# RWKV substitution: rows of the 16-blocks spread over their partitions through DRAM instead of by shuffles

## The chip, the cores and the metric

One core of a Trainium2 chip runs the whole program. The metric is the device time of one execution in microseconds, as the median of several runs. The engines are PE (TensorE, matrix products), PEld (its weight loads), DVE (VectorE), ACT (ScalarE), POOL (GpSimd) and SP, which here only issues transfers. Each engine runs its own instructions in the order in which they were placed on it; it waits at an instruction until what that needs is there, and everything behind it on that engine waits too.

## What is computed

One residual block over 256 tokens of width 2048, in f32: RMS norm, one wide input projection, RWKV-7 time mixing (16 heads of 64) and latent attention side by side, gates and an output projection, then a gated MLP and an input embedding. The change lies in the RWKV part. Cut to what matters of the reference:

```python
def rwkv7_scan(r, decay, k, v, kk, a):
    def step(state, inp):                      # 256 steps, state 64 x 64 per head
        r_t, w_t, k_t, v_t, kk_t, a_t = inp
        sa = jnp.einsum('bhvk,bhk->bhv', state, -kk_t)
        state = (state * w_t[:, :, None, :]
                 + sa[..., None] * (kk_t * a_t)[:, :, None, :]
                 + v_t[..., None] * k_t[:, :, None, :])
        y_t = jnp.einsum('bhvk,bhk->bhv', state, r_t)
        return state, y_t
    ...
u = rms_norm(h, pre_mix_norm[i])
z = u @ w_in[i]
z_rw, z_mla, z_gate = jnp.split(z, (RW_COLS, RW_COLS + MLA_COLS), axis=-1)
...
mix = (g_rw * (y_rw @ w_branch_rw[i]) + g_mla * (y_mla @ w_branch_mla[i])) @ w_out[i]
```

## The kernel before

**The scan in chunks.** The 256 steps are done as 4 chunks of 64 (`NCH`, `C`). Inside a chunk the steps depend on each other through a 64 x 64 triangular matrix for each head, `n`. Its inverse is needed. It is built from the inverses of its 16 x 16 blocks on the diagonal: those come by substitution, column after column, and the larger blocks by products (`ph`, `px`).

**Tiles.** A pair is two heads, on partitions 0 to 63 and 64 to 127. `rw_pair(J, j, ...)` is a generator for pair `j` of 8. Two pairs run side by side as one round, `par` 0 and 1, so there are four rounds. The substitution is done once for both: the second pair (`par == 1`) issues it for a tile that holds both. `dg` (128 partitions x 128 elements) holds the diagonal blocks of both pairs and all four chunks: every 16 partitions are the 16 rows of a block, and the 16 elements in a row stand side by side. `xc` of the same shape takes the inverse and starts as the identity.

**Rows for everybody.** To eliminate in column `t`, every partition of a block needs all rows of that block. They are kept in `rp16`, 16 x 128 elements on each partition. Fifteen instructions fill it: shuffle `i` copies row `i` of each 16-partition group to the 16 partitions of its group. Row 15 isn't needed and holds ones. The columns then are two DVE instructions each, a product into `pd` and a sum into `xc`; each depends on the one before. `pd` shares its memory with `dg` (tag `dg`, one buffer).

**Dense work between.** The matrix products of the projections are another generator, `dense_work`. It yields once for each block of 128 rows of weights: 6 matmuls of 256 columns, the planner's unit. `rw_pair` yields after each of its steps a length in such units, and the loop behind `duo` advances `dense_work` by as many. So `SUB = 1.56` units stand behind each step of the substitution, `STEP = 2.4` behind other steps. This sets the order in which instructions are made; a scheduler then places them on each engine by what is ready when, with evacuations ahead.

**Weights.** `wchunk` loads 128 x 1024 f32 on SP's queue into `raw` (3 buffers). For each half, ACT rounds it into `hi` (L148) and DVE subtracts for the remainder `lo` (L149), in 5 buffers each. One such half serves two units, 12 matmuls (L183 to L185: hi times hi, hi times lo, lo times hi). So DVE has to make one `lo` for each half-chunk that TensorE goes through, and whatever holds DVE holds these.

**Names around it.** L848 makes `dg` ready for the substitution. L866 and L867 split weights of the pair's output gate (`lgs`, from `lwr`), L735 those of the next pair (`lws`). L992, L999 and L162 finish the pair before (`yf`, `yrw`). L362 mixes neighbouring tokens of a new projection (`z`). L871 and L888 are the first steps behind the columns (`Xc`, `YH`), L893 and L897 the products' halves on DVE. L730 is ACT's load of `lwr` for a later pair.

Of the kernel before, what the change touches and what calls it, by code (L numbers as in the profile page):

```python
# [8 lines left out]
F32 = mybir.dt.float32  # L9
# [7 lines left out]
P = 128  # L17
# [8 lines left out]
NH = 8  # L26
DS = float(np.exp(-0.5))

STEP, CHUNK, SUB = 2.4, 2.8, 1.56


NONE, READY, FREE, HOLD, AHEAD, TAIL = 0, 2, 3, 5, 6, 7
# [76 lines left out]
def hybrid_block(tc, A):  # L109
    nc = tc.nc  # L110
# [199 lines left out]
    es_e = ExitStack()  # L310
# [7 lines left out]
    def e2(nm, shape=None, dt=F32):  # L318
        return mp.tile(shape or [P, 2 * T], dt, name=nm, tag="e2", bufs=17)
# [261 lines left out]
    for i in range(2):  # L581
        p = slice(64 * i, 64 * i + 64)
# [22 lines left out]
    for j in range(2):  # L605
        ps = run(dense(cq, [A["w_q"][4 + j]], 4))
        o, b = e2("upo", [P, 2, T]), e2("qps", [P, 2, T])
# [94 lines left out]
    es_e = ExitStack()  # L702
# [2 lines left out]
    Xbs, krs = [[ep.tile([P, NCH, 2, C], F32, name=f"{nm}{i}") for i in range(2)] for nm in ("Xb", "kb")]  # L705
    for n in Xbs + krs:
        nc.gpsimd.memset(n[:], 0.0)
    rp16 = ep.tile([P, 16, 2 * NCH * 16], F32, name="rp16")
    nc.gpsimd.memset(rp16[:, 15, :], 1.0)

# [3 lines left out]
    def rw_pair(J, j, k, r, v):  # L714
        par = j % 2
# [95 lines left out]
        n = ep.tile([P, NCH, C], F32, name=f"n{par}", bufs=1)  # L811
# [29 lines left out]
        dg, xc = J["dg"], J["xc"]  # L841
# [3 lines left out]
        if par == 1:  # L845
            d8, x8 = [a[:].rearrange("p r c j -> p (r c) j") for a in (dg, xc)]
            act(x8, i16, AF.Copy)
            tt(out=d8, in0=i16, in1=d8, op=ALU.subtract)  # L848
        yield NONE, SUB

        for o in range(0, 15, 3):
            if par == 1:
                for i in range(o, o + 3):
                    nc.vector.stream_shuffle(out=rp16[:, i, :], in_=dg[:].rearrange("p r c j -> p (r c j)"),
                                             mask=[i] * 16 + [16 + i] * 16)
            yield NONE, SUB
        for t in range(1, 16):
            if par == 1:
                pd = ep.tile([P, 2 * NCH, 16], F32, name="pd", tag="dg", bufs=1)
                r8 = rp16[:].rearrange("p i (q j) -> p q i j", j=16)  # L860
                tt(out=pd[:, :, 0:t + 1], in0=x8[:, :, 0:t + 1], in1=r8[:, :, 0:t + 1, t], op=ALU.mult)
                nc.vector.tensor_reduce(out=x8[:, :, t], in_=pd[:, :, 0:t + 1], axis=AX.X, op=ALU.add)
            yield NONE, SUB
        lgs = ep.tile([P, 3, P], F32R, name="lgs", bufs=2)
        act(lgs[:, 0:2, :], lwr[:, 2:4, :], AF.Copy)
        tt(out=lgs[:, 2, :], in0=lwr[:, 2, :], in1=lgs[:, 0, :].bitcast(F32), op=ALU.subtract)  # L866
# [47 lines left out]
        for h in range(2):  # L914
# [4 lines left out]
            o = pb[:, 0:T].rearrange("p (c n) -> p c n", c=NCH)  # L919
# [15 lines left out]
        for c in range(NCH):  # L935
# [3 lines left out]
            o = lambda i, h, hs: pc[hs, i * P + h * C:i * P + h * C + C]  # L939
# [97 lines left out]
    def duo(q):  # L1037
        while len(zz[q]) < 3:
            next(work)
        J = {}  # L1040
        return [rw_pair(J, 2 * q + c, *[z[:, c, :] for z in zz[q]]) for c in range(2)]
# [176 lines left out]
    with tc.tile_pool(name="fw", bufs=2) as fw, tc.tile_pool(name="psu", bufs=3, space=PSUM, reuse_waits="tile") as psu:  # L1218
# [30 lines left out]
        for n, (j, q) in enumerate([(j, q) for q in range(4) for j in range(3)] + [(j, q) for j in range(3, NFF) for q in range(4)]):  # L1249
# [12 lines left out]
            if (j, q) == (0, 3):  # L1262
# [5 lines left out]
                r = st[:, 26:28]  # L1268
# [177 lines left out]
```

## Time and profile before

| | |
|---|---|
| median of 3 runs | 1561.18 us (1561.16 to 1561.9) |
| the profiled execution | 1560.39 us, span 1558.6 us |
| granted TensorE clock | 0.997 |
| shuffles, L854 | 60, 297 ns median, 228.1 to 505.0 us |
| the column's product, L861 | 60, 285 ns median, 233.1 to 519.9 us |
| the column's sum, L862 | 60, 226 ns median |
| mean DMA rate | 183 GB/s |

The profile is of one execution and so compares with its own 1560.39 us. Times in it are from the start of its span. Engines overlap: an engine's idle time costs only where another waits for it. A matmul is listed with its full length of some 0.28 us though the next starts 0.12 us behind it, so that short waits of TensorE are covered by busy time.

### The profile page before, as it was taken

Reading aid. Unit: us, or ns where it says so; the run is one execution under the profiler, and the core shown is the slowest. Engines: PE = TensorE matmul, PEld = TensorE weight load, DVE = VectorE, ACT = ScalarE, POOL = GpSimd, SP = SyncE. Lnnn points to the kernel's source line nnn. Section 1 sums busy time; section 2 is a strip of 40 time slices with the busy share of each in tenths; the row PEclk is TensorE's granted clock in tenths of the full one; section 3 lists DMA queues with packets and bytes.
Section 4 is the critical chain, followed back from the end, with each engine's and each line's share of the span. In section 5 each row is a group of like instructions: output and inputs, shape, how many; then the busy total and the mean of one; then the engine's idle time right before and its main releaser. Section 6 shows DMA issues by size and latency. Waiting matters only on the chain.

```text
span 1558.6 us, 29636 instructions
## 1 busy us (share of the span) xinstructions
PE 1538.0 (99%) x10850; PEld 1388.3 (89%) x10850; DVE 1182.2 (76%) x2670; ACT 942.1 (60%) x1944; POOL 60.9 (4%) x125
## 2 busy tenths in 40 slices
PE   9999999999999999999999999999999999999997
PEld 9989999999999999887888888888888888888886
DVE  7896687898989776557787777777777655777866
ACT  7686756566565555456766555555655555776653
POOL 0000201101011102000000000000000000000000
PEclk9999999999999999999999999999999999999998
DMA  8654555454444546865656555565655666666564
GB/s 304 192 172 141 154 173 164 138 171 129 147 150 136 160 153 200 306 199 167 203 174 205 198 181 202 179 203 179 206 181 190 175 192 195 197 197 191 166 200 148
DMA packets 80482, 285.19 MB, mean 183 GB/s; under 512 B 9040, under 2 KB 10320, under 8 KB 80336
## 3 DMA queue, kind: packets, MB, share of 16 engines
q1 hardware_dynamic: 77760, 279.48, 56.3%
q10 hardware_dynamic: 2576, 3.81, 0.7%
q8 instruction: 85, 1.39, 0.4%
q14 instruction: 61, 0.50, 0.1%
HBM read 281.16 MB, written 2.10 MB: 182 GB/s over the span
## 4 chain that ended last, share of the span: by engine, by line
PE 89%; DVE 6%; ACT 2%; DMA 1%; issue 1%; DVEq 0%; ACTq 0%
PE d L170 21%; PE d L174 11%; PE d L183 9%; PE d L185 8%; PE d L184 8%; PE o L196 7%; PE o L198 6%; PE o L200 6%; PE e L196 2%; PE e L198 2%; PE e L200 2%; DVE lo L149 2%; ACT hi L148 1%; DMA raw<-in_w_in 1%; PE tr L237 0%
## 5 line engine op out<-in xcount | busy, mean ns | idle before, releaser
L149 DVE TENSOR_TENSOR lo<-raw,hi 128x512 fp32r<-128x512 f32 x684 | 461.0, 690 | 213.9 <-ACT hi L148 208.5
L148 ACT CAST hi<-raw 128x512 fp32r<-128x512 f32 x684 | 410.7, 619 | 297.9 <-PE o L200 97.9
L183 PE MATMUL d<-uT,hi 128*128 128x256 f32 x1072 | 307.7, 287 | 0.7 <-ACT hi L161 0.6
L170 PE MATMUL d<-u,highs 128*128 128x512 f32 x1312 | 305.5, 390 | 0.0
L185 PE MATMUL d<-uT,lo 128*128 128x256 f32 x1072 | 300.5, 280 | 0.7 <-DVE lo L162 0.2
L184 PE MATMUL d<-uT,hi 128*128 128x256 f32 x1072 | 299.6, 279 | 0.1
L170 PEld LDWEIGHTS d<-u,highs 128*128 128x128 f32 x1312 | 243.3, 188 | 48.9
L148 ACT CAST highs<-raw 128x512 fp32r<-128x512 f32 x328 | 186.8, 616 | 115.0 <-DMA raw<-in_w_up 80.3
L183 PEld LDWEIGHTS d<-uT,hi 128*128 128x128 f32 x1072 | 201.7, 188 | 2.8 <-ACT hi L161 0.8
L185 PEld LDWEIGHTS d<-uT,lo 128*128 128x128 f32 x1072 | 201.5, 188 | 2.1 <-DVE lo L149 1.1
L184 PEld LDWEIGHTS d<-uT,hi 128*128 128x128 f32 x1072 | 201.7, 188 | 0.4 <-DVE uT L290 0.3
L149 DVE TENSOR_TENSOR hi<-raw,highs 128x512 fp32r<-128x512 f32 x164 | 112.7, 688 | 76.8 <-PE d L174 58.8
L174 PE MATMUL d<-u,lo 128*128 128x256 f32 x752 | 117.7, 280 | 0.0
L149 DVE TENSOR_TENSOR lo<-raw,highs 128x512 fp32r<-128x512 f32 x164 | 112.0, 684 | 0.0
L174 PE MATMUL d<-u,hi 128*128 128x256 f32 x656 | 103.3, 279 | 0.0
L174 PEld LDWEIGHTS d<-u,lo 128*128 128x128 f32 x752 | 101.7, 188 | 0.8
L174 PEld LDWEIGHTS d<-u,hi 128*128 128x128 f32 x656 | 91.5, 188 | 3.5
L198 PE MATMUL o<-lo,fsplit 128*128 128x512 f32 x264 | 88.6, 389 | 0.0
L196 PE MATMUL o<-hi,fsplit 128*128 128x512 f32 x264 | 88.5, 389 | 0.0
L200 PE MATMUL o<-hi,fsplit 128*128 128x512 f32 x264 | 88.4, 389 | 0.0
L1228 ACT ACTIVATE cy<-d 128x512 f32<-128x512 f32 x44 | 26.2, 597 | 67.8 <-PE d L174 67.8
L198 PEld LDWEIGHTS o<-lo,fsplit 128*128 128x128 f32 x264 | 49.6, 188 | 10.7 <-DVE lo L149 0.3
(389 smaller groups left out, 2550.9 us busy)
## 6 DMA issues: line engine op xcount, KB each, us to landing
raw<-in_w_up SPq DMA_DIRECT2D x176, 512.0 KB, 4.3
raw<-in_w_in SPq DMA_DIRECT2D x133, 512.0 KB, 3.6
raw<-in_w_down SPq DMA_DIRECT2D x88, 512.0 KB, 4.3
raw<-in_w_out SPq DMA_DIRECT2D x32, 512.0 KB, 4.4
raw<-in_w_pg SPq DMA_DIRECT2D x32, 512.0 KB, 3.6
raw<-in_w_bm SPq DMA_DIRECT2D x16, 512.0 KB, 3.7
raw<-in_w_br SPq DMA_DIRECT2D x16, 512.0 KB, 3.7
raw<-in_w_kv SPq DMA_DIRECT2D x8, 512.0 KB, 3.6
```

What stands on the lines that cost most here:

```text
L148: nc.scalar.copy(hi[:], raw[:, c:c + 512])
L149: tt(out=lo[:], in0=raw[:, c:c + 512], in1=hi[:].bitcast(F32), op=ALU.subtract)
L170: mm(ps[:, c, :], hi(i, col, P), mov[i][2], start=first and x == 0 and i == 0, stop=False)
L174: mm(ps[:, c, 0:T], lo(i, col, P), mov[i][0], start=False, stop=last and x == len(parts) - 1 and i == len(mov) - 1)
L183: mm(ps[:, c, :], hi(i, col, P), mov[i][:, 0:T], start=f, stop=False)
L184: mm(ps[:, c, :], hi(i, col, P), mov[i][:, T:2 * T], start=False, stop=False)
L185: mm(ps[:, c, :], lo(i, col, P), mov[i][:, 0:T], start=False, stop=l)
L196: mm(b[:], h, hi(i, g * 512, 512), start=f, stop=False)
L198: mm(b[:], h, lo(i, g * 512, 512), start=False, stop=False)
L200: mm(b[:], x, hi(i, g * 512, 512), start=False, stop=l)
L1228: act(y[:], ps[:, :, 0:T], AF.Copy)
```

## The change

The fifteen shuffles go. ACT issues a transfer that writes `dg` to DRAM (`rows16`, 128 x 128 f32, 64 KB). POOL issues one that reads it back: each partition gets the 15 x 128 elements of the first fifteen rows of its block in one piece of 7,680 bytes, and the 16 partitions of a block all read the same piece. Where five steps of the substitution held the shuffles, six empty steps follow. The steps of the columns are 1.45 units long and no longer 1.56.

```diff
-STEP, CHUNK, SUB = 2.4, 2.8, 1.56
+STEP, CHUNK, SUB, COL = 2.4, 2.8, 1.56, 1.45
...
+    rows16 = es_e.enter_context(tc.tile_pool(name="dr", bufs=1, space=bass.MemoryType.DRAM)).tile([P, P], F32, name="rows16")
     rp16 = ep.tile([P, 16, 2 * NCH * 16], F32, name="rp16")
...
         yield NONE, SUB
-
-        for o in range(0, 15, 3):
-            if par == 1:
-                for i in range(o, o + 3):
-                    nc.vector.stream_shuffle(out=rp16[:, i, :], in_=dg[:].rearrange("p r c j -> p (r c j)"),
-                                             mask=[i] * 16 + [16 + i] * 16)
+        if par == 1:
+
+            nc.scalar.dma_start(rows16[:], dg[:].rearrange("p r c j -> p (r c j)"))
+            nc.gpsimd.dma_start(rp16[:, 0:15, :].rearrange("p i n -> p (i n)"),
+                                bass.AP(rows16.tensor, rows16.offset, [[16 * P, 8], [0, 16], [1, 15 * P]]))
+        for _ in range(6):
             yield NONE, SUB
         for t in range(1, 16):
             if par == 1:
...
-            yield NONE, SUB
+            yield NONE, COL
```

The new lines make later line numbers one higher: L848 becomes L849, L861 L862, L862 L863, L148 and L149 stay. In the rows below `rp_2510` and `rp_2513` are `rp16`, and `rows_2512` is `rows16`.

DVE in the first round, from `dg` made ready to the first columns, before:

```order
L848 TENSOR_TENSOR dg<-cst,dg 128x128
L149 TENSOR_TENSOR lo<-raw,hi 128x512
L854 STREAM_SHUFFLE rp_2510<-dg 128x128 x5
L149 TENSOR_TENSOR lo<-raw,hi 128x512
L854 STREAM_SHUFFLE rp_2510<-dg 128x128 x4
L149 TENSOR_TENSOR lo<-raw,hi 128x512
L854 STREAM_SHUFFLE rp_2510<-dg 128x128 x4
L149 TENSOR_TENSOR lo<-raw,hi 128x512
L854 STREAM_SHUFFLE rp_2510<-dg 128x128 x2
L861 TENSOR_TENSOR pd<-xc,rp_2510 128x8x2
L862 TENSOR_REDUCE xc<-pd 128x8
L149 TENSOR_TENSOR lo<-raw,hi 128x512
```

And after:

```order
L849 TENSOR_TENSOR dg<-cst,dg 128x128
L149 TENSOR_TENSOR lo<-raw,hi 128x512 x5
L362 SCALAR_TENSOR_TENSOR z_3270<-d,vec,z_3270 128x255
L149 TENSOR_TENSOR lo<-raw,hi 128x512
L362 SCALAR_TENSOR_TENSOR z_3270<-d,vec,z_3270 128x255
L862 TENSOR_TENSOR pd<-xc,rp_2513 128x8x2
L863 TENSOR_REDUCE xc<-pd 128x8
L862 TENSOR_TENSOR pd<-xc,rp_2513 128x8x3
L149 TENSOR_TENSOR lo<-raw,hi 128x512
```

Six `lo` stand between `dg` and the first column where four stood, and the first column now needs the read. In the later rounds L999 (now L1000) has also moved ahead of the first column.

ACT in the second round, from before the write to the loads of `lwr`, after:

```order
L148 CAST hi<-raw 128x512 x2
L853 DMA rows_2512<-dg 128x128
L148 CAST hi<-raw 128x512
L991 ACTIVATE yf<-pm,vec 128x256 x2
L148 CAST hi<-raw 128x512
L361 ACTIVATE z_4723<-d,omu 128x256
L148 CAST hi<-raw 128x512
L361 ACTIVATE z_4723<-d,omu 128x256
L866 ACTIVATE lgs<-lwr 128x256 x2
L148 CAST hi<-raw 128x512
L731 DMA lwr<-in_w_lora 128x512
L148 CAST hi<-raw 128x512
```

Before, the same piece read:

```order
L148 CAST hi<-raw 128x512 x3
L990 ACTIVATE yf<-pm,vec 128x256 x2
L148 CAST hi<-raw 128x512
L361 ACTIVATE z_4740<-d,omu 128x256
L148 CAST hi<-raw 128x512
L361 ACTIVATE z_4740<-d,omu 128x256
L865 ACTIVATE lgs<-lwr 128x256 x2
L148 CAST hi<-raw 128x512
L730 DMA lwr<-in_w_lora 128x512
```

The write stands between two casts and waits for DVE's L849; the rest of ACT's order is the same.

POOL in the first round, after; ahead of the change the row of the DMA was not there:

```order
L798 COPY bk_2912<-bk_2912 64x4x64
L798 COPY bk_2916<-bk_2916 64x4x64
L854 DMA rp_2513<-rows_2512 128x1x1920
L901 COPY Xb_2502<-Xc_3557 32x4x32 x4
L901 COPY Xb_2503<-Xc_3563 32x4x32 x4
```

The read stands ahead of POOL's copies of the substitution's result (before: L900). SP's order of transfers is unchanged.

## The prediction

> **What bounds the kernel now.** I read the page first, then the stretches around the four substitutions, then the DVE's groups and its order in time there, and last the landings of transfers. A count after x is how often a row stands.
>
> ```profile
> span 1558.6 us, 29636 instructions
> ...
> PE 1538.0 (99%) x10850; PEld 1388.3 (89%) x10850; DVE 1182.2 (76%) x2670; ACT 942.1 (60%) x1944; POOL 60.9 (4%) x125
> ...
> PE 89%; DVE 6%; ACT 2%; DMA 1%; issue 1%; DVEq 0%; ACTq 0%
> ```
>
> TensorE is the bound over the whole program: 89% of the chain that ended last is its own. A change on DVE pays only where the chain leaves TensorE for DVE. The profiled execution took 1560.39 us with a span of 1558.6; the median of the runs is 1561.18, so I add the differences to that. The table of stretches (columns: length; then busy time of PE, PEld, DVE, ACT and POOL; clock, DMA share, GB/s) cuts out the four rounds, one for each two pairs of heads, from the end of L848 to the transposes behind the columns:
>
> ```profile
> 227.60:252.00 24.40, 24.40 (x212) 24.40 (x210) 23.35 (x86) 11.25 (x21) 0.00 (x0) 1.00 0.57 175
> 317.40:347.00 29.60, 29.14 (x377) 28.39 (x374) 27.71 (x103) 15.73 (x34) 0.00 (x0) 1.00 0.62 181
> 408.00:439.00 31.00, 29.88 (x381) 28.39 (x379) 29.22 (x104) 15.73 (x31) 0.18 (x1) 1.00 0.59 186
> 499.60:529.00 29.40, 29.01 (x378) 28.46 (x380) 26.28 (x96) 16.63 (x31) 0.00 (x0) 1.00 0.52 169
> sum 114.40, PE 112.43 PEld 109.64 DVE 106.56 ACT 59.34 POOL 0.18; mean PE 28.11 PEld 27.41 DVE 26.64 ACT 14.84 POOL 0.04
> ```
>
> In the rounds DVE is busy 106.6 of 114.4 us: here, and hardly elsewhere, it is as full as TensorE. Yet TensorE idles only 114.40 - 112.43 = 1.97 us in all four, none of it in round 1. So relief of DVE can return about 2 us, a little more if waits shorter than one matmul stand hidden in busy time. That is below 0.2% (3.1 us), which is about what a measurement of this kernel tells from no change.
>
> What DVE does in round 1, by groups:
>
> ```profile
> L149 DVE TENSOR_TENSOR lo<-raw,hi 128x512 fp32r<-128x512 f32 x18 | 12.1, 679 | 0.0
> L861 DVE TENSOR_TENSOR pd<-xc,rp 128x16 f32<-128x16 f32 (+14 forms) x15 | 4.3, 289 | 0.4
> L854 DVE STREAM_SHUFFLE rp<-dg 128x128 f32<-128x128 f32 x15 | 3.5, 294 | 0.0
> L862 DVE TENSOR_REDUCE xc<-pd 128x8 f32<-128x16 f32 (+14 forms) x15 | 3.4, 227 | 0.3
> ```
>
> **The change, part by part.**
>
> *Shuffles removed.* 15 shuffles a round; successive ones start about 0.21 us apart though each lasts 0.294, so a round saves 15 x 0.21 = 3.1 us of DVE, 12.4 us in all. What of it reaches the end is bounded by the 1.97 us above. Little does even so: the six steps in which DVE is now free stand before the first column, and DVE cannot work ahead there, because lo waits for hi and hi for TensorE to give a buffer back. These ACT rows show that pace:
>
> ```profile
> 228.05 0.62 ACT L148 CAST hi<-raw 128x512 fp32r<-128x512 f32 x1 [0.46 <-PE d L184]
> ...
> 229.45 0.62 ACT L148 CAST hi<-raw 128x512 fp32r<-128x512 f32 x1 [0.78 <-PE d L184]
> ```
>
> One half-chunk, the work of one hi and one lo, lasts TensorE 1.40 us, which is two of the planner's units; a SUB is 1.09 us.
>
> *Columns closer.* 15 x 1.45 = 21.75 units of cover instead of 23.4, with the same columns. A column costs DVE 289 + 227 = 516 ns; per half-chunk there are 1.38 columns instead of 1.28, so DVE falls behind by 0.05 us more on each of some 11, 0.5 us a round; but the columns end 0.8 half-chunk earlier and DVE's load is lighter behind them. I take zero and keep +0.5 a round for the range. The sixth step balances it: 6 x 1.56 + 21.75 + 1.56 = 32.67 units a round against 32.76.
>
> *The round trip added.* ACT issues a write of 64 KB, POOL waits for it and issues a read of 128 x 7,680 B = 983 KB, and the first column waits for that. Neither transfer has a row. Nearest rows (KB each, median us from issue to landing) and the weight queue's packets, MB and share:
>
> ```profile
> q1 hardware_dynamic: 77760, 279.48, 56.3%
> ...
> raw<-in_w_in SPq DMA_DIRECT2D x133, 512.0 KB, 3.6
> ...
> lwr<-in_w_lora ACTq DMA_DIRECT2D x8, 256.0 KB, 3.0
> ...
> gbc<-in_g_pm SPq DMA_DIRECT2D x2, 512.0 KB, 5.3
> ...
> gple<-in_g_pl SPq DMA_DIRECT2D x2, 512.0 KB, 7.1
> ...
> out<-h ACTq DMA_DIRECT2D x4, 256.0 KB, 2.2
> ```
>
> The write: 2.2 (out, the only writes to DRAM) to 3.0 us (lwr, on ACT's queue beside the weights); I take 2.3. The read: 279.48 MB in 56.3% of 1558.6 us is 318 GB/s with all engines busy, so the 459 KB beyond a 512 KB transfer add 1.4 us: 3.6 + 1.4 = 5.0 at least, 7.1 + 1.4 = 8.5 at most, and 5.3 + 1.4 = 6.7 by gbc, which like this read repeats a piece of DRAM over partitions while weights flow. I take 6.7. POOL's own start: below nothing beyond the landing times, above 1.3 us, the longest issue in the trace (below); I take 0.5. So the data lands 9.5 us after L848 ends, with ends at 7.2 and 12.8.
>
> ```profile
> L1134 SPq DMA_DIRECT2D gple<-in_g_pl x2: 432/872/1312, 645.9 to 648.6; - x2
> ```
>
> The Trainium skill's "DMA: Bandwidth & Descriptors", Anatomy of one DMA, fits a GpSimd transfer with 2.0 us plus bytes over 436 GB/s. By that the read would take 4.3 us, the landing would be near 7, and this sum would be zero. The trace speaks against it: for 512 KB the fit gives 3.2 us, the rows 3.6 to 7.1.
>
> *When it is too late.* DVE in order of time in rounds 1 to 4: L848, the first column, and the lo that the new order puts behind its first columns.
>
> ```profile
> 227.26 0.29 DVE L848 TENSOR_TENSOR dg<-cst,dg 128x128 f32<-128x128 f32 x1
> ...
> 233.10 0.19 DVE L861 TENSOR_TENSOR pd<-xc,rp 128x16 f32<-128x16 f32 x1
> ...
> 236.37 0.68 DVE L149 TENSOR_TENSOR lo<-raw,hi 128x512 fp32r<-128x512 f32 x1
> ...
> 317.10 0.28 DVE L848 TENSOR_TENSOR dg<-cst,dg 128x128 f32<-128x128 f32 x1
> ...
> 325.12 0.18 DVE L861 TENSOR_TENSOR pd<-xc,rp 128x16 f32<-128x16 f32 x1
> ...
> 407.65 0.29 DVE L848 TENSOR_TENSOR dg<-cst,dg 128x128 f32<-128x128 f32 x1
> ...
> 417.98 0.69 DVE L149 TENSOR_TENSOR lo<-raw,hi 128x512 fp32r<-128x512 f32 x1
> ...
> 499.29 0.29 DVE L848 TENSOR_TENSOR dg<-cst,dg 128x128 f32<-128x128 f32 x1
> ...
> 505.79 0.18 DVE L861 TENSOR_TENSOR pd<-xc,rp 128x16 f32<-128x16 f32 x1
> ...
> 507.12 0.69 DVE L149 TENSOR_TENSOR lo<-raw,hi 128x512 fp32r<-128x512 f32 x1
> ...
> 508.49 0.28 DVE L866 TENSOR_TENSOR lgs<-lwr,lgs 128x128 fp32r<-128x128 f32 x1
> 508.69 0.42 DVE L162 TENSOR_TENSOR yrw<-yf,yrw 128x256 fp32r<-128x256 f32 x1
> 509.03 0.22 DVE L861 TENSOR_TENSOR pd<-xc,rp 128x40 f32<-128x40 f32 x1
> 509.17 0.68 DVE L149 TENSOR_TENSOR lo<-raw,hi 128x512 fp32r<-128x512 f32 x1
> ```
>
> Behind the waiting column stand all further lo, and TensorE needs one every 1.40 us. I ask at which landing the next lo ends where it ends now; from there on both versions do the same work. Round 1: six lo stand ahead of the column (two now, with shuffles between); the seventh, now ended at 237.05, comes 1.3 us behind the landing (two columns' pieces and itself): 235.75, or 8.2 us after L848. TensorE did not wait in this round, so I allow it 0.8 more: 9.0. Round 2: the order behind the first column is unchanged, so 325.12: 7.7. Round 3: two L999 and a split have moved ahead of the column; the lo that ended at 418.67 comes 1.9 us behind the landing (the column's product and sum, two lgs and a split, each 0.2 to 0.34 from start to start, and lo itself): 416.8, or 8.8. Round 4: likewise 2.0 us, against 507.81, which gives 6.2; the lo after it, now ended at 509.85, comes 3.6 us behind, which gives 6.7; I take 6.6. At 9.5 the four rounds lose 0.5 + 1.8 + 0.7 + 2.9 = **5.9 us**, each a wait of TensorE, since DVE is too full behind it to catch up.
>
> *What waits with it.* The write stands on ACT right behind L848's end, when ACT has its casts done or waits for them; up to 0.5 us in rounds 3 and 4, hidden by the lead of hi. In rounds 2 to 4 the reload of lwr on ACT waits for a DVE reader that stands behind the first column, and hi casts behind that reload. Such a wait is there already (who waited for whom, in round 2's window and, for POOL, over the span):
>
> ```profile
> ACT hi L148 <- DVE pd L861: 2.5, 2, 1.5
> ...
> POOL Xb L900 <- DVE Xc L897: 179.4, 4, 48.1
> ```
>
> One hi stands ahead of it, so lo remains the later of the two: nothing extra. POOL has only L900's copies behind its read, which wait for the columns anyway. SP's order is the same; its weight reloads meet 4 x 1.05 MB more traffic at 52 to 62% DMA share, which is in the 5.3-based read, and two chunks in hand cover the reverse.
>
> **Sum:** 1560.39 + 5.9 = 1566.3 for the profiled execution, 1567.1 beside the median.
>
> **Rivals.**
>
> *Hidden after all.* The landing at 7.2 to 8: rounds 1 and 3 lose nothing, 2 and 4 gain or lose under 1 us: 1559.5 to 1562.5, say 1561. For it: the lower rows (2.2, 3.6). Against it: it needs both.
>
> *Half the engines.* The read's source counts 8 outermost, each repeated 16 times. If that spreads the transfer over 8 of 16 engines, 983 KB take 6.2 instead of 3.1 us, and the landing goes to 12.6: 3.6 + 4.9 + 3.8 + 6.0 = 18.3 us, 1579.5. Every transfer of the trace counts 128 outermost, so no row speaks for or against. The Trainium skill states such a rule on the same page, Rules for kernel authors: an outermost count below 16 keeps a transfer to at most so many engines. No run here shows it yet.
>
> *Faster.* The read lands before DVE comes to the first column, 5.6 to 6.5 us after L848 by the same counting; then 3.1 us of DVE's work a round is gone where TensorE did wait. The place is the end of rounds 2 to 4:
>
> ```profile
> PE px L882 <- DVE YH L893: 1.7, 4, 0.6
> ```
>
> That and shorter waits give back 2 to 3.5 us: 1558. It decides if the landing is under 6.5, below my lowest sum.
>
> **How the numbers follow.** Exposed by 1 to 3 us a round 0.38, hidden 0.34, half the engines 0.20, faster 0.08. A sixth of the exposed case stays within 0.2%: slower 0.32 + 0.20 = 0.52, same 0.34 + 0.06 = 0.40, faster 0.08. I predict the likeliest, 1567; its own range is 1563 to 1573. The range for all is 1559 to 1578: below it lies part of the faster case, above it half of that on 8 engines. As cases of both kinds hold much of the chance, it is wide.
>
> **What would show it.** In the new profile: no shuffles; the read landing 6 to 8 us after POOL issues it and the first column starting 9 to 10 us after L848; TensorE idle in each round right behind that, 0.5 to 3 us; waits of pd for the transfer of 3 to 4 us, four times. If pd waits under 1 us, the landing is mis-sized and the time is the old one. If it waits over 6, the engines are halved. If pd waits 3 us and TensorE does not, my account of the lead of lo is wrong.

## The result, and the profile after

The changed kernel takes 1597.67 us (median of 4 runs, 1596.8 to 1598.29), the kernel before 1561.17 us beside it: 36.5 us more, ratio 1.0233, 95% interval 1.0219 to 1.0247. The profiled execution took 1598.29 us. From its page: the span, the engines, the queue of the read, the chain that ended last, and the group of matmuls with lo.

```profile
span 1596.5 us, 29545 instructions
...
PE 1545.3 (97%) x10850; PEld 1394.7 (87%) x10850; DVE 1171.4 (73%) x2550; ACT 943.5 (59%) x1944; POOL 63.5 (4%) x129
...
q0 software_dynamic: 1088, 3.93, 1.1%
...
PE 85%; DVE 6%; DMA 6%; ACT 2%; issue 1%; DVEq 0%; ACTq 0%; POOLq 0%
...
L185 PE MATMUL d<-uT,lo 128*128 128x256 f32 x1072 | 303.8, 283 | 28.2 <-DVE lo L149 28.0
```

DVE did lose its shuffles (2670 to 2550 instructions, 10.8 us of busy time), and TensorE has the same 10850 matmuls. But TensorE now idles 1596.5 - 1545.3 = 51.2 us where it idled 20.6, and the chain has 6% DMA where it had 1%. q0 is new: it is the read, 3.93 MB in four rounds.

The stretches of 30 us behind L849 (L848 before) in the four rounds, columns as in the prediction:

```profile
227.60:257.60 30.00, 21.29 (x169) 21.09 (x169) 14.63 (x42) 8.87 (x16) 0.76 (x1) 0.89 0.55 144
329.60:359.60 30.00, 23.32 (x198) 22.80 (x195) 17.99 (x56) 11.43 (x24) 0.59 (x1) 0.89 0.60 158
429.60:459.60 30.00, 24.15 (x207) 23.76 (x206) 18.93 (x57) 12.68 (x25) 0.58 (x1) 0.89 0.58 171
528.50:558.50 30.00, 23.48 (x206) 22.96 (x202) 18.15 (x54) 12.37 (x24) 0.58 (x1) 0.89 0.54 145
sum 120.00, PE 92.23 PEld 90.61 DVE 69.70 ACT 45.35 POOL 2.50; mean PE 23.06 PEld 22.65 DVE 17.43 ACT 11.34 POOL 0.62
```

TensorE is busy 92.2 of 120 us there, 27.8 us idle against 1.97 in the rounds of before. DVE, as full as TensorE in the rounds of before, is now busy 58%: it waits. The granted clock is 0.89 where it was 1.00.

Who waited for whom over the span (total us, times, longest), and the transfers (KB each, median us from issue to landing):

```profile
DVE pd L862 <- DMA rp<-rows: 43.1, 4, 13.0
PEld d L185 <- DVE lo L149: 29.4, 7, 8.9
PE d L185 <- DVE lo L149: 28.0, 6, 8.7
ACT hi L148 <- DMA raw<-in_w_in: 26.4, 11, 7.2
ACT hi L148 <- DVE pd L862: 17.8, 4, 11.5
...
rp<-rows POOLq DMA_DIRECT2D x4, 960.0 KB, 12.5
...
rows<-dg ACTq DMA_DIRECT2D x4, 64.0 KB, 3.2
```

The columns wait 43.1 us for the read, four times. TensorE waits 28.0 us for lo, which stands behind the first column on DVE; in all four rounds that is the wait with which its stall ends. The row with raw will matter: hi waited 19.1 us for these weights before, 26.4 now. Round 1 in order of time:

```profile
227.07 0.29 DVE L849 TENSOR_TENSOR dg<-cst,dg 128x128 f32<-128x128 f32 x1
...
227.39 0.33 ACTq L853 DMA_DIRECT2D rows<-dg  x1
...
230.80 0.76 POOL L854 DMA_DIRECT2D rp<-rows  x1 [21.36 <-DMA rows<-dg]
...
241.72 1.14 ACT L148 CAST hi<-raw 128x512 fp32r<-128x512 f32 x2 [6.18 <-DMA raw<-in_w_in]
246.80 0.18 DVE L862 TENSOR_TENSOR pd<-xc,rp 128x16 f32<-128x16 f32 x1 [13.00 <-DMA rp<-rows]
...
247.05 0.62 ACT L148 CAST hi<-raw 128x512 fp32r<-128x512 f32 x1 [4.19 <-DVE pd L862]
...
247.34 0.69 DVE L149 TENSOR_TENSOR lo<-raw,hi 128x512 fp32r<-128x512 f32 x1
...
248.08 0.58 PE L185 MATMUL d<-uT,lo 128*128 128x256 f32 x1 [8.71 <-DVE lo L149]
...
248.46 0.41 PE L183 MATMUL d<-uT,hi 128*128 128x256 f32 x1
```

L849 ends at 227.36; the first column starts 19.4 us later, and 16.3, 15.9 and 15.2 us in rounds 2 to 4. Two things happen at once: the column waits 13 us for its rows, and ahead of that ACT waits 6.2 us for weights. A third comes behind: the first matmul after the stall of 8.71 us lasts 0.58 us and the next ones 0.41, instead of 0.28. The clock of those stretches (next to last columns, before DMA share and GB/s) stands at half:

```profile
244.41:251.22 6.81, 3.14 (x14) 3.14 (x15) 4.11 (x16) 1.24 (x2) 0.00 (x0) 0.50 0.16 34
343.39:350.20 6.81, 2.85 (x13) 2.86 (x14) 4.26 (x18) 2.17 (x4) 0.00 (x0) 0.50 0.36 106
445.79:452.60 6.81, 5.38 (x25) 5.38 (x26) 6.45 (x24) 3.00 (x7) 0.00 (x0) 0.50 0.62 189
541.37:548.17 6.80, 2.82 (x13) 2.82 (x14) 4.45 (x17) 1.14 (x2) 0.00 (x0) 0.50 0.33 105
sum 27.23, PE 14.20 PEld 14.20 DVE 19.27 ACT 7.54 POOL 0.00; mean PE 3.55 PEld 3.55 DVE 4.82 ACT 1.89 POOL 0.00
```

So far: four stalls of 8.71, 6.68, 5.85 and 6.18 us, together 27.4, and 14.2 us of matmuls at half clock, which at full clock would have taken about half, so they cost at most 7.1. That makes up to 34.5 of the 36.5 us. Whether the late column, the late weights or both made the stalls the trace can't say: in round 1 they end 5 us apart.

### The profile page after: what moved, and what is told of

It is laid out like the page before. It is cut to its first block, busy times and chain, and to the rows that moved or that the text cites. A ratio compares the mean times of both kernels' runs of the same rounds, so it can differ in the third digit from the quotient of the medians.

```text
span 1596.5 us, 29545 instructions
## 1 busy us (share of the span) xinstructions
PE 1545.3 (97%) x10850; PEld 1394.7 (87%) x10850; DVE 1171.4 (73%) x2550; ACT 943.5 (59%) x1944; POOL 63.5 (4%) x129
## 3 DMA queue, kind: packets, MB, share of 16 engines
q0 software_dynamic: 1088, 3.93, 1.1%
## 4 chain that ended last, share of the span: by engine, by line
PE 85%; DVE 6%; DMA 6%; ACT 2%; issue 1%; DVEq 0%; ACTq 0%; POOLq 0%
PE d L170 20%; PE d L174 10%; PE d L183 8%; PE d L185 8%; PE d L184 7%; PE o L200 6%; PE o L196 6%; PE o L198 6%; DMA rp<-rows 3%; PE e L196 2%; PE e L198 2%; PE e L200 2%; DVE lo L149 2%; DMA raw<-in_w_in 1%; ACT hi L148 1%
## 5 line engine op out<-in xcount | busy, mean ns | idle before, releaser
L149 DVE TENSOR_TENSOR lo<-raw,hi 128x512 fp32r<-128x512 f32 x684 | 460.8, 690 | 218.9 <-ACT hi L148 213.0
L148 ACT CAST hi<-raw 128x512 fp32r<-128x512 f32 x684 | 411.4, 619 | 346.2 <-PE o L200 107.7
L185 PE MATMUL d<-uT,lo 128*128 128x256 f32 x1072 | 303.8, 283 | 28.2 <-DVE lo L149 28.0
L148 ACT CAST highs<-raw 128x512 fp32r<-128x512 f32 x328 | 186.9, 617 | 110.0 <-DMA raw<-in_w_up 78.0
L185 PEld LDWEIGHTS d<-uT,lo 128*128 128x128 f32 x1072 | 204.7, 191 | 29.9 <-DVE lo L149 29.2
L183 PEld LDWEIGHTS d<-uT,hi 128*128 128x128 f32 x1072 | 204.9, 191 | 2.4 <-ACT hi L161 0.4
L184 PEld LDWEIGHTS d<-uT,hi 128*128 128x128 f32 x1072 | 204.7, 191 | 0.5 <-DVE uT L290 0.4
L149 DVE TENSOR_TENSOR hi<-raw,highs 128x512 fp32r<-128x512 f32 x164 | 112.7, 688 | 78.2 <-PE d L174 61.6
L149 DVE TENSOR_TENSOR lo<-raw,highs 128x512 fp32r<-128x512 f32 x164 | 111.9, 684 | 0.0
L198 PEld LDWEIGHTS o<-lo,fsplit 128*128 128x128 f32 x264 | 49.6, 188 | 10.6 <-DVE lo L149 0.3
```

The lines of the kernel that those rows point to most:

```text
L148: nc.scalar.copy(hi[:], raw[:, c:c + 512])
L149: tt(out=lo[:], in0=raw[:, c:c + 512], in1=hi[:].bitcast(F32), op=ALU.subtract)
L183: mm(ps[:, c, :], hi(i, col, P), mov[i][:, 0:T], start=f, stop=False)
L184: mm(ps[:, c, :], hi(i, col, P), mov[i][:, T:2 * T], start=False, stop=False)
L185: mm(ps[:, c, :], lo(i, col, P), mov[i][:, 0:T], start=False, stop=l)
L198: mm(b[:], h, lo(i, g * 512, 512), start=False, stop=False)
```

## The experiments

Times are medians; the kernel before, run beside each, took 1561.15 to 1561.44 us. The code gives the main lines of each change, against after; shuf_big and shuf_big128 are given against shuf, and experiment 4 changes one line of shuf_big.

**1. The parts that aren't the transfer.** *spacing* keeps the shuffles and takes only the sixth step and COL; *no_trip* has neither shuffles nor transfers; its columns read zeros, and so they start right behind the diagonal's last step.

```
 spacing:  +  for o in range(0, 15, 3): ... three stream_shuffle ...; yield NONE, SUB
           -  nc.scalar.dma_start(rows16...); nc.gpsimd.dma_start(rp16...)
 no_trip:  -  both dma_start;  r8 = a tile of zeros, memset once
```

> The shuffles of before, with the sixth step and the closer columns of after, no transfer. Theory (the wait for the transfer costs it all): 1560 to 1563 us. Rival (closer columns hold up lo, or the shift of work by the planner costs): 1567 us or more, up to 1597 if that is all of it.

> Neither shuffles nor transfers; the columns read a tile of zeros set once (wrong values), six steps and closer columns as after. It shows how much relief of DVE is worth at most. Theory (TensorE idled 1.97 us in the four rounds of before): 1558 to 1562 us. Rival (waits below one matmul hide more): 1550 to 1557 us.

Measured: spacing 1562.76 us (ratio 1.0010, interval 1.0000 to 1.0019), no_trip 1557.62 (0.9975, 0.9966 to 0.9985). The sixth step and the closer columns cost 1.4 us (0 to 3); no_trip came out 0.4 us under its range, and puts the relief of DVE at 3.8 us at most. So the change could win some 0.25% at best.

**2. The engines, the bytes and the delay of the read, with the column waiting for it.** *outer128* reads as many bytes with another outermost count, the first block's rows for every partition; *small* reads 1/15 of the bytes, one row that all columns use; *delay* puts two copies in DRAM between write and small read.

```
 outer128: -  [[16 * P, 8], [0, 16], [1, 15 * P]]
           +  [[0, P], [1, 15 * P]]
 small:    +  nc.gpsimd.dma_start(rs16[:], AP(rows16, [[16 * P, 8], [0, 16], [1, P]]))   # columns read rs16
 delay:    +  nc.gpsimd.dma_start(hop0[:], rows16[:]); nc.gpsimd.dma_start(hop1[:], hop0[:])   # then small's read, from hop1
```

> The read's source is named as 128 x 7,680 B (its first block's rows for every partition, so seven of eight blocks get wrong rows) instead of 8 x 16 x 7,680 B; bytes, destination and the order of all instructions stay. Theory (8 of 16 engines carry the read): its packets are spread over 16 engines, the landing falls from 12.5 us to 6 to 8 us behind its issue, the first column starts 10 to 12 us behind the end of the diagonal's last step instead of 15 to 19, and by the prediction's four break-evens (9.0, 7.7, 8.8, 6.6 us) the time is 1568 to 1578 us. Rival (memory, the common source rows or POOL's queue set the pace, engines don't): landing about 12.5 us again and 1595 to 1600 us.

> The round trip stays, but the read brings one row of 512 B to each partition (64 KB instead of 960 KB) and all columns use that row, so the substitution's values are wrong. Theory (the read's bytes on half the engines set the landing): it lands 2 to 3.5 us behind its issue, first column 6.5 to 8.5 us behind the diagonal's last step, TensorE waits under 1 us a round, 1560 to 1566 us. Rival (the fixed cost of write, POOL's start and read sets it): landing still over 8 us, first column 13 us or more behind, 1585 us or more.

> Late data without bytes: the write of 64 KB, two copies of 64 KB from DRAM to DRAM, one behind the other, then a read of 64 KB (one row of 512 B for each partition, which all columns use, so the values are wrong). DVE's order is that of after but for one lo more ahead of the first columns. The landing should come 14 to 18 us behind the diagonal's last step, as in after, with 1/15 of its bytes. Theory 1 (the late first column alone costs landing less break-even, as the prediction counts, about 1.4 us less for the lo more): 7 + 8 + 7 + 9 less 5, so 1582 to 1600 us. Rival 2 (the 36 us of after were the starved weights, the column's wait adds little): 1575 us or less.

Measured: outer128 1574.16 us (1.0083, 1.0068 to 1.0098), small 1568.68 (1.0049, 1.0034 to 1.0064), delay 1575.45 (1.0084, 1.0069 to 1.0100). Of outer128, its read and its waits:

```profile
rp<-rows POOLq DMA_DIRECT2D x4, 960.0 KB, 6.8
...
DVE pd L862 <- DMA rp<-rows: 18.1, 4, 5.5
```

The same 960 KB land in 6.8 instead of 12.5 us, and 23.5 of the 36.5 us are gone, with the same order of instructions. In the trace's packet records after seldom has more than 8 packets of the read in flight (11 at the most), of 471 ns (median of round 1); outer128 reaches 16 to 19, of 291 ns. That the read ran on 8 engines is inferred from this count, as the records name no engine. That is the first theory as expected. small was 2.7 us over its range: its columns stand 6 lo earlier in the four rounds, presumably since the planner takes a small read for quicker. delay missed its range by 6.6 us, and fell at the edge of its rival's: its data came 13.7, 14.5, 15.2 and 11.8 us after the diagonal, a little less than meant, and 6 lo more stand ahead of the columns, where the expectation had counted 4. It comes back below.

**3. The bytes with nobody waiting.** *small_big* issues small's read and behind it the full read, unread. *shuf* does 15 shuffles into one row that all columns read; *shuf_big* adds the change's two transfers, unread; *shuf_big128* names their source as outer128 does. The order on DVE is the same in the three.

```
 shuf:        nc.vector.stream_shuffle(out=rs16[:], ...)   x15, no transfers
 shuf_big:    + nc.scalar.dma_start(rows16...)
              + nc.gpsimd.dma_start(rp16[:, 0:15]..., AP(rows16, [[16 * P, 8], [0, 16], [1, 15 * P]]))   # unread
 shuf_big128: the same with [[0, P], [1, 15 * P]]
```

> As the kernel with the small read, and behind that read POOL issues the full read of 960 KB as well, into a tile that nobody reads (wrong values as there). Theory (only the wait costs; 4 MB beside the weights cost nothing by themselves): within 3 us of the kernel with the small read alone. Rival (contention with the weight stream delays raw, so hi and lo): 1575 us or more, with hi waiting for raw in each round.

> Control for the next two: no transfers; 15 shuffles as before, but all into one tile of one row, which all columns read (the values of the substitution are wrong); six steps and closer columns as after. All theories: 1561 to 1566 us, as the kernel with the change's spacing alone (1562.76).

> As the control (wrong values as there), and in each round the change's write of 64 KB and read of 960 KB are issued as well, into a tile that nobody reads; so nothing on DVE, ACT or TensorE waits for them. Theory A (the read sits on 8 of 16 engines in front of weight packets, and a weight transfer needs all 16, so raw comes late): 8 to 25 us over the control, with hi waiting for raw and TensorE for lo in the rounds. Rival B (the transfers cost only where a column waits for them and has used up the lead): within 3 us of the control.

> As the one before (wrong values as there), with the source of the unread read named as 128 x 7,680 B, so that it spreads over 16 engines. Theory A: within 4 us of the control. Rival C (it is the bytes that cost, on however many engines): the same as the one before, within 3 us. Rival B: as the control, like the one before.

Measured: small_big 1589.96 us (1.0180, 1.0163 to 1.0197), so 21.3 over small, and the theory that the bytes alone cost nothing fell. shuf 1560.25 (0.9994, 0.9984 to 1.0003), shuf_big 1590.00 (1.0183, 1.0166 to 1.0200), shuf_big128 1562.55 (1.0008, 0.9998 to 1.0017). **A transfer for which nobody waits costs 29.8 us on 8 engines and 2.3 us on 16.** The 29.8 are more than the 8 to 25 expected, and shuf itself came out 0.8 us under its range. The waits and the order of time in shuf_big, round 1:

```profile
ACT hi L148 <- DMA raw<-in_w_in: 36.2, 13, 9.7
...
239.80 10.45 SPq L141 DMA_DIRECT2D raw<-in_w_in  x2
...
247.07 3.09 ACT L148 CAST hi<-raw 128x512 fp32r<-128x512 f32 x5 [9.66 <-DMA raw<-in_w_in]
247.72 0.69 DVE L149 TENSOR_TENSOR lo<-raw,hi 128x512 fp32r<-128x512 f32 x1 [6.89 <-ACT hi L148]
247.75 0.58 PE L183 MATMUL d<-uT,hi 128*128 128x256 f32 x1 [4.24 <-ACT hi L148]
```

There is no wait for the read. ACT waits 9.7 us for one weight tile, then casts five hi in a row, and TensorE had to wait 4.24 us for the first (and starts again at half clock, 0.58 us). Over the span hi waits 36.2 us for these weights, against 8.7 in shuf and 16.5 in shuf_big128. The weight tiles that SP issued from 230 to 247 us show why, in shuf, shuf_big and shuf_big128 in this order:

```profile
DMA to landing us min/median/max: 3.5/3.5/4.4
```

```profile
DMA to landing us min/median/max: 3.5/10.4/12.9
```

```profile
DMA to landing us min/median/max: 3.4/4.1/6.2
```

Beside the read on 8 engines a weight tile takes up to 12.9 us to land, beside the one on 16 up to 6.2. The stretch of 30 us in round 1 of shuf_big, then of shuf_big128:

```profile
228.00:258.00 30.00, 25.76 (x199) 25.33 (x199) 21.93 (x84) 10.71 (x20) 0.75 (x1) 0.89 0.65 164
```

```profile
228.00:258.00 30.00, 29.21 (x364) 28.76 (x363) 27.29 (x98) 14.20 (x28) 1.34 (x4) 1.00 0.72 223
```

With 8 engines the core moves 164 GB/s, read and weights together, with 16 engines 223.

**4. Engines or addresses.** outer128 changed the count of engines and also the source, from 64 KB of DRAM to one piece of 7.5 KB. Four kernels cross the two: shuf_big with only the source's access pattern changed.

```
 near8:     [[16, 8],  [0, 16], [1, 15 * P]]
 near16:    [[16, 16], [0, 8],  [1, 15 * P]]
 near4:     [[16, 4],  [0, 32], [1, 15 * P]]
 spread128: [[112, P], [1, 15 * P]]
```

> As the control with shuffles and an unread transfer on 8 blocks x 16 (1590.00 us; wrong values as there), with the 8 source blocks 64 B apart instead of 8 KB, so that nearly the same 7,680 B are read 128 times. Theory A (8 of 16 engines carry the read): 1583 to 1593 us, 8 packets in flight, each about 600 ns. Rival D (it was the spread of the source over 64 KB of DRAM that made packets slow, as in the kernel with two copies): 1560 to 1568 us, packets near 291 ns.

> As the control with shuffles and an unread transfer on an outermost 128 (1562.55 us; wrong values as there), with the 128 source rows 448 B apart, so that they spread over 64 KB as in after. Theory A (engines): 1560 to 1567 us, packets near 291 ns. Rival D (spread of the source): 1575 to 1592 us, packets 450 ns or more.

> The control with shuffles and an unread read (wrong values as there), its source named as 16 blocks 64 B apart, each repeated 8 times. Theory A (what counts is how many engines the outermost count allows; 16 are all there are): 1560 to 1567 us, up to 16 packets in flight, near 291 ns. Rival (blocks of 8 neighbouring partitions in a row on one engine are slow as well, which would be why the kernel with two copies took 1584.66 us): 1572 us or more, packets about 500 ns.

> The same with 4 blocks, each repeated 32 times. Theory A: 4 packets in flight, 32 packets an engine, so 9.3 us at least and some 20 us beside weights; the weights are held up about twice as long as with 8 blocks (26 to 30 us there over four rounds): 1605 to 1660 us. Rival (the loss is that of the bytes or of POOL's queue, not of the count of engines): 1580 to 1595 us, as with 8.

| outermost count, source | time, us | ratio to before (interval) | read, issue to landing, us |
|---|---|---|---|
| 4, near (near4) | 1607.18 | 1.0303 (1.0283 to 1.0323) | 24.1 |
| 8, near (near8) | 1587.51 | 1.0166 (1.0149 to 1.0182) | 14.3 |
| 8, over 64 KB (shuf_big) | 1590.00 | 1.0183 (1.0166 to 1.0200) | 14.6 |
| 16, near (near16) | 1565.69 | 1.0030 (1.0020 to 1.0040) | 8.6 |
| 128, one piece (shuf_big128) | 1562.55 | 1.0008 (0.9998 to 1.0017) | 7.0 |
| 128, over 64 KB (spread128) | 1561.57 | 1.0000 (0.9991 to 1.0009) | 7.1 |
| no transfer (shuf) | 1560.25 | 0.9994 (0.9984 to 1.0003) | |

The spread of the source changes nothing that can be measured; the outermost count sets both the landing and what the weights lose. The rows of the reads of near4 and near8:

```profile
rp<-rows POOLq DMA_DIRECT2D x4, 960.0 KB, 24.1
```

```profile
rp<-rows POOLq DMA_DIRECT2D x4, 960.0 KB, 14.3
```

16 is a little worse than 128: up to 16 packets are in flight in both, but their median is 385 to 546 ns against 291. Why is open. The queue's count of packets (1088 in after, 576 in outer128) holds, besides the 512 of the reads' data, small ones of 4 bytes, 128 more a read on 8 engines than on 16; at 7 ns each (median) they come to about 0.1 us an engine and can hardly be the cause.

**5. Versions whose columns get all their own rows.** *copies* writes the diagonal twice, so that the read counts 16 outermost. *hybrid6* shuffles rows 0 to 5 and transfers rows 6 to 14 in that way, *hybrid6_8* with one write on 8. *hybrid9* and *hybrid9_8* do so for rows 9 to 14, and give the columns' product a buffer of its own.

```
 copies:  for c in range(2): nc.scalar.dma_start(AP(rows16, offset c*16*P, [[32 * P, 8], [P, 16], [1, P]]), dg)
          nc.gpsimd.dma_start(rp16[:, 0:15]..., AP(rows16, [[16 * P, 16], [0, 8], [1, 15 * P]]))
 hybrid6: six stream_shuffle;  the read of rp16[:, 6:15], 9 * P each
 hybrid9: nine stream_shuffle; the read of rp16[:, 9:15], 6 * P each;  pd: tag="dg" removed
```

> All rows by the transfer, with right values, on 16 engines: the diagonal blocks are written twice to DRAM, so that the read's source counts 16 blocks, each repeated 8 times. Theory (as the read of 128 x 7,680 B): landing 6 to 8 us behind its issue, 1571 to 1578 us. Rival (only an outermost count of 128 spreads it, or the second write delays the read): 1585 us or more.

> Rows 0 to 5 by six shuffles as before, rows 6 to 14 by the transfer (576 KB on 16 engines, from two copies in DRAM), needed first by the sixth column; right values. Theory: no column waits, weights are hardly held up, and 9 of 15 shuffles a round are gone, so between the kernel without either (1557.62) and before: 1558.5 to 1562 us. Rival (the sixth column still waits, or the bytes cost): 1565 us or more.

> As the one before with the write once and the read on 8 blocks x 16 (so 8 engines by theory). Theory A (8 engines starve the weights in proportion to the bytes beyond what the lead covers): 1563 to 1580 us, hi waiting for raw in the rounds. Rival (9 packets of 0.6 the size leave the weights room): within 2 us of the one on 16 engines.

> Rows 0 to 8 by nine shuffles, rows 9 to 14 by the transfer (384 KB, two copies in DRAM, source 16 x 8), and the columns' product in a buffer of its own, so that the first column needn't wait until the write has read the diagonal's buffer (it waited 2.3 us there in the kernel with six shuffles). Right values. Theory (that wait and the wait of the sixth column cost the 12 us there): 1558.5 to 1563 us. Rival (the second write on ACT and 384 KB beside the weights cost as much): 1566 us or more.

> As the one before, with one write and the read on 8 blocks x 16. Right values. Theory A (8 engines starve the weights by their share of the bytes, 384 of 960 KB, some of which the lead covers): 1562 to 1572 us. Rival (below the lead nothing is lost): 1558.5 to 1561.5 us.

Measured: copies 1584.66 us (1.0148, 1.0134 to 1.0162), hybrid6 1573.32 (1.0075, 1.0063 to 1.0088), hybrid6_8 1580.26 (1.0119, 1.0105 to 1.0132), hybrid9 1561.93 (1.0002, 0.9994 to 1.0011), hybrid9_8 1562.09 (1.0007, 0.9998 to 1.0016). copies missed: its two writes let POOL issue the read only 4.4 to 5.6 us after L849's step (2.1 to 4.3 in outer128), and the read takes 8.5 instead of 6.8, as near16's does. hybrid6 missed too; its waits:

```profile
DVE pd L870 <- DMA rp<-rows: 5.8, 3, 2.7
DVE pd L870 <- DMA rows<-dg: 5.8, 4, 2.3
```

The second row is a wait that nobody had planned: the product pd takes over dg's buffer, so the first column waits until the write has read dg. In after it stood hidden behind the longer wait. hybrid9 has neither wait and comes out even with before: nine of fifteen shuffles back, and nothing won. Its two changes were made together, so their shares are open; hybrid6_8 is 6.9 us over hybrid6, which fits the 8 engines, although it also writes once only; it is 0.3 us over its range. hybrid9_8 can't be told from hybrid9, and lies where its two ranges nearly meet: 384 KB on 8 engines cost nothing that can be measured, so the loss doesn't follow the bytes alone. No version here beats before by what can be measured.

## Why the prediction was wrong

The direction and the place were right: four stalls behind the first column, the order on DVE, lo behind pd. The size was short by 30 us. Step by step:

**The landing (the term that failed first).** "The data lands 9.5 us after L848 ends"; it was 15.2 to 19.4. The write was taken at 2.3 us from the rows with 2.2 and 3.0 and took 3.2. POOL issued the read 0.3 to 0.5 us after the write had landed, as taken. The read was taken at 6.7 and took 12.5 (12.0 to 16.0) from its issue; 1.3 to 2.75 us of that went by before its first packet moved. The rival with half the engines had the right mechanism at 0.20 and the wrong price: it doubled the bytes' time alone, 3.1 to 6.2 us, and came to a landing of 12.6. The read's 16 packets an engine need 16 x 291 ns = 4.7 us on 8 engines; beside the weights they took 10 to 12. The nearest rows all counted 128 outermost, and the prediction said so, but still took the likeliest from them. The Trainium skill's "DMA: Bandwidth & Descriptors", Why a DMA increments its semaphore by 16 and not by 1, takes the largest count up to 16 that divides the slowest dimensions of both access patterns. The cross of 4, 8, 16 and 128 above agrees: most often 4, 8, 16 and 16 of the read's packets are in flight, with peaks two or three higher.

**The weights (the omitted term).** "Two chunks in hand cover the reverse" was costed at nothing. shuf_big measured it by itself: 29.8 us. small_big is nearly the case that was predicted, data 10.2, 8.0, 7.9 and 8.1 us after the diagonal's step, beside the full read on 8 engines; it still lost 28.6 us. Rows that come in time would thus not have been enough for the prediction, as long as such a read runs beside the weights. That the tiles land late is shown (12.9 us against 4.4 at the most in round 1); how the read holds them up is argued: a tile lands when the last of its engines is done, and half of them would alternate with read packets. The Trainium skill's "DMA: Bandwidth & Descriptors", Queues, rings and completion order, says that an engine takes turns between its queues. The traces give no engine numbers, so no run here shows it directly.

**When it is too late (right in the main).** The four break-evens of 9.0, 7.7, 8.8 and 6.6 us can be tried on the measured starts of the first columns:

| kernel | first column after the diagonal's step, rounds 1 to 4 | sum over the break-evens | measured loss |
|---|---|---|---|
| after | 19.4, 16.3, 15.9, 15.2 | 34.7 | 36.5 |
| copies | 14.8, 12.0, 14.2, 13.5 | 22.4 | 23.4 |
| outer128 | 11.2, 11.0, 10.6, 9.0 | 9.7 | 12.8 |
| delay (6 lo more ahead, 8.4 less) | 13.7, 14.5, 15.2, 11.8 | 14.7 | 14.2 |
| small (6 lo fewer ahead, 8.4 more) | 7.8, 7.7, 7.0, 5.8 | 4.6 | 7.3 |

The account of lo's lead holds within about 3 us, in delay and small without any bytes to speak of. ("Two now" in round 1 should read four, as the order of before shows; no figure hangs on it.) In after the agreement is in part luck: by the count TensorE should have waited 34.7 us, but its four stalls come to 27.4, and the half clock behind them, which the count doesn't have, fills most of the gap. So after has two causes, of which each alone would cost most of the loss: the late column, 35 by this count, and the starved weights, 30 as measured in shuf_big. The 35 stay an estimate, as no run held the column back for so long without the bytes. The two overlap in time and come to 36.5 together. A cure must take both away: outer128 took away the second and shortened the first, and kept 12.8.

**What was left out.** The half clock after a stall: at most 7.1 us. And ACT: the prediction had "nothing extra" for hi behind the reload of lwr; hi waited 17.8 us for the columns on DVE where it had waited 3.3, 11.5 of them in one piece right behind that reload in round 2. This falls in the same time as DVE's own wait; what it costs by itself no run shows.

**Relief and spacing (right).** Relief was put at 2 to 3.5 us and is 3.8 at most (no_trip); closer columns were taken as 0 to 2 us and cost 1.4. "If it waits over 6, the engines are halved" held: pd waited 43.1 / 4 = 10.8 us.

## What to carry to other kernels

Look at the outermost count of a transfer's access pattern before its bytes: a broadcast that names 8 blocks x 16 repeats rode on half the engines by its packets in flight, and delayed the weight stream, which cost 29.8 us with nobody waiting for the read, of 36.5 with a reader. When a transfer is added beside a stream that feeds the bound engine, price two things apart, its own landing and the stream's delay; a copy of it that nobody reads measures the second in one run. And bound the prize first: all shuffles gone were worth 0.25%, which a round trip through DRAM with one late wait a round can't pay.

## What the runs showed of the hardware

- 7,680 B took 291 ns a packet on the undisturbed engine, and 4,096 B of weights 159 ns, which is 26 GB/s in both. Beside the weights on 8 engines the read's packets took 435 to 561 ns (medians of the rounds of after).
- In after, each stall of TensorE (5.85 to 8.71 us) was met by one stretch of 6.8 us at a granted clock of 0.50, which began 2 to 5 us into the stall and lasted into the work behind it. The Trainium skill's "TensorE: Matmul & The Clock Gate", What's actually happening, gives half clock after an idle window of about 3.4 us and full clock after a busy one as long. The trace agrees, at two such windows each time; in the other runs these stretches lasted 3.41, 6.83, 10.24 or 17.07 us, each a multiple of 3.41.
- A write of 64 KB to DRAM took 3.2 us, and each of the further hops of 64 KB 3.0 to 3.6 us from issue to landing (delay): four small ones in a row take about as long as one read of 960 KB on 8 engines.
- In after the 8-engine read lands in 12.5 us; in shuf_big, where no column waits for it and more weights flow beside it while it runs (98 against 79 GB/s on average), in 14.6.
